# A streaming encoder layer on one NeuronCore: the split weights' homes moved by 16 bytes

## The chip, the cores and the metric

The kernel runs on one core of a Trainium2 chip. The metric is the device time of one execution in microseconds (us). Engines are named as the profile names them: PE (TensorE, matmul), PEld (its weight loads), DVE (VectorE), ACT (ScalarE), POOL (GpSimd), SP (the engine that issues most DMAs). L145 is line 145 of the kernel before.

## The reference, cut to what matters

One layer of a hybrid encoder is computed for 1024 prompt tokens and 64 sample tokens (1088 columns in all) of width 1024, in float32. Each matmul of the reference is dense:

```python
rq, rk, rv, rg, sq, sk, sv, ga, gb = split(rms_norm(x, g_attn) @ w_in)
a = (rms_norm(retention(rq, rk, rv)) * silu(rg)) @ w_ret_out
b = sliding_window_attention(sq, sk, sv) @ w_swa_out
x = x + (sigmoid(ga) * a + sigmoid(gb) * b) @ w_mix_out
x = x + cross_attention(rms_norm(x, g_cross) @ w_cq, mem @ w_mk, mem @ w_mv) @ w_co
x = x + (silu(rms_norm(x, g_ffn) @ w_gate) * (rms_norm(x, g_ffn) @ w_up)) @ w_down
y = rms_norm(x, g_final)
```

Retention keeps a state of 256x256 per head (4 heads) and is worked through in blocks. For the sample tokens the states and key/value caches come in as inputs. The outputs are y, the new states, the last keys and values, and the memory's keys and values.

## The kernel before, in words

**Two parts for each operand.** Float32 operands are split into two parts in the type float32r: `hi`, a rounded copy that ACT writes (L123), and `lo`, the rest, which DVE writes as source minus hi (L124). A product is then three matmuls that add up in PSUM: hi·hi, hi·lo and lo·hi. `mm3` (L147 to L151) does that for one weight block of 128x128 and one stretch of columns.

**Weights.** A weight matrix comes in tiles named `raw` (128 partitions x 1024 numbers, two homes, loaded by SP). The split writes tiles named `wq`, made by `new_op` (L145): 128 partitions x 2 x 512 numbers, the first 512 being hi and the other 512 lo. A pool named "weights" holds the two raw homes and five wq homes in the projection phase and six afterwards. Each 128 columns of a wq tile are the stationary operand of matmuls.

**Strassen.** The large matrices (w_in's parts, w_gate, w_up, w_down) are multiplied by a seven-product scheme. `weight_ops` (L165) forms five of the seven weight sums, with POOL adding and subtracting raw halves in place (L183 to L189), and splits each into a wq tile. `multiply` (L197) is one product: for each of four blocks k of 128 rows it issues six matmuls over 272 columns, two column halves c in two PSUM banks: hi·hi and hi·lo for c = 0, the same for c = 1 (L205, L206 each time), and lo·hi for both (L208). The moving operands are tiles B11, T1 and so on in two rings of eight homes at the right end of SBUF.

**The phases.** `project_phase` multiplies w_in; between its products stands `retention` (L711), head by head, and later `memory_phase` (L485), which computes the memory's keys and values. `mix_phase` does the windowed attention with w_ret_out's products as filler, then w_swa_out and w_mix_out; `cross_phase` and `cross_out_phase` do the cross-attention; `ffn_phase` the gated feed-forward with w_gate, w_up and w_down, and `finish` the last norm.

**Retention's small tiles.** For the sample tokens each head loads kf and qf (128x2x64) and writes sf (64x64). Before, kf shares the home tagged "sf" with the block loop's sf tile, qf has a home tagged "qsm" and the small sf one tagged "sfs" (L777, L790). `bias_table` uses the tag "sf" too.

**The memory phase's small tiles.** Eight pieces of the memory come in through two homes tagged "mraw" (L493); results leave through four homes tagged "mo" (L490).

**What sets the order.** The program is written as a list of steps in Python; the tile framework's scheduler simulates a timeline and orders the instructions of each engine, except where `issue_after` fixes a place. So a tile with another home, or one that shares a home, can change the order. SBUF homes are given out in steps of 32 bytes per partition; in the built program of before, the raw homes start at bytes 8128 and 12224 and the wq homes at 16320, 20416, 24512, 28608, 32704 and (the sixth) 36800. All of these leave the remainder 0 when divided by 64. The ring tiles all leave 32, retention's tiles 0.

Of the kernel before, what the change touches and what calls it, by code (L numbers as in the profile page):

```python
# [11 lines left out]
F32 = mybir.dt.float32  # L12
F32R = mybir.dt.float32r
# [6 lines left out]
P = 128  # L20
# [3 lines left out]
SMP = 64  # L24
# [6 lines left out]
NMEM = 256  # L31
# [78 lines left out]
class Kernel:  # L110
# [31 lines left out]
        return parts  # L142

    def new_op(self):
        return self.wp.tile([P, 2, 512], F32R, tag="wq", bufs=self.wbufs, name="wq")  # L145

    def mm3(self, ps, wh, wl, xh, xl, start, stop):  # L147
        mm = self.nc.tensor.matmul
# [333 lines left out]
    def memory_phase(self, mp):  # L482


        nc, tc, io = self.nc, self.tc, self.io  # L485
        g_mem = self.gains[:, 4, :]
        mr = self.mem.enter_context(tc.tile_pool(name="mr", bufs=1, reuse_waits="tile", side="right"))
        ms = self.ms = [mr.tile([P, 2, NMEM], F32R, name=f"ms{k}") for k in range(KT)]
        macc = mp.tile([P, NMEM], F32, name="macc")
        out = lambda: mp.tile([P, NMEM], F32, tag="mo", bufs=4, name="mo")  # L490
        room = lambda: mp.tile([P, 1024], F32, tag="mw", bufs=3, name="mw")
        for k in range(KT):
            x = mp.tile([P, NMEM], F32, tag="mraw", bufs=2, name="mraw")  # L493
            self.load(x, io["memT"][:, k, :])
            self.gained(ms[k], 0, NMEM, x, g_mem, k)
            if k:
                nc.scalar.activation(x, x, AF.Square)
                nc.vector.tensor_tensor(out=macc, in0=macc, in1=x, op=ALU.add)
            else:
                nc.scalar.activation(macc, x, AF.Square)  # L500
            if k % 2:
                yield
        self.token_rstd(self.mtok, [macc], self.spans(NMEM), D)
        yield
        self.spread(macc, self.mtok)
        for m in range(KT):
            ps = self.dense(self.unit(io["w_mk"][m], KT, room=room), ms, 0, NMEM)
            o = out()
            nc.vector.tensor_tensor(out=o, in0=ps, in1=macc, op=ALU.mult)
            self.store(self.d_mk[m // 2, :, m % 2, :], o)  # L510
            self.store(io["o_mk"][m], o)
            yield
        for h in range(H - 1):
            us = [self.unit(io["w_mv"][h, i], 4, 256, room) for i in range(2)]
            for t in range(2):
                ps = self.dense_psum()
                for k in range(KT):
                    x = ms[k][:, :, t * P:(t + 1) * P]
                    self.mm3(ps[:, :256], x[:, 0], x[:, 1], *us[k // 4][k % 4], k == 0, k == KT - 1)
                o = out()  # L520
                nc.scalar.mul(o, ps[:, :256], self.mtok[:, t:t + 1])
                self.store(self.d_mv[h, :, t, :], o)
                self.store(io["o_mv"][t * P:(t + 1) * P, h * 256:(h + 1) * 256], o)
            yield
# [177 lines left out]
    def retention(self, h):  # L702
        nc, io = self.nc, self.io
        mm = nc.tensor.matmul
        ra = self.ra
# [7 lines left out]
        for b in range(NBLK):  # L713
# [28 lines left out]
            sf = ra.tile([P, BLK + P], F32, tag="sf", bufs=1, name="sf")  # L742
# [31 lines left out]
        self.store(io["o_rsp"][h].rearrange("(t p) e -> p t e", p=P), state)  # L774

        s0, vf = new("state"), new("vf")
        kf, qf = (ra.tile([P, 2, SMP], F32, tag=tag, bufs=1, name=tag) for tag in ("sf", "qsm"))  # L777
        self.load(s0, io["cstate"][h].rearrange("(t p) e -> p t e", p=P))
        vf = vf[:, :, :SMP]
        for j, x in ((1, kf), (2, vf), (0, qf)):  # L780
# [6 lines left out]
        pss = self.bank("psss")  # L787
        for dt in range(2):
            mm(pss[:SMP, 0, :SMP], kf[:, dt, :], qf[:, dt, :], start=dt == 0, stop=dt == 1)
        sf = ra.tile([P, SMP], F32, tag="sfs", bufs=1, name="sfs")  # L790
        nc.vector.scalar_tensor_tensor(sf[:SMP], pss[:SMP, 0, :SMP], self.rtok[:SMP, 8:], dm[:SMP, BLK + P:],
                                       ALU.mult, ALU.mult)
        po = self.bank("pos")
# [903 lines left out]
```

## Time and profile before

| what | before |
|---|---|
| time, median of 3 runs | 2240.6 us (2237.51 to 2248.04) |
| the profiled execution's own time | 2239.58 us |
| its span, first to last instruction | 2237.8 us |
| PE busy | 2171.3 us, 97% |
| PEld busy | 2106.8 us, 94% |
| DVE busy | 1600.4 us, 72% |
| ACT busy | 884.7 us, 40% |
| POOL busy | 690.5 us, 31% |
| mean granted PE clock | 0.986 |

In a row of the groups view, "out<-in" names the tiles by the program's names, "x1832" is the count, and the numbers behind the bar are the group's busy time in us and the mean duration of one in ns. Matmuls are pipelined and their ends are modelled: a matmul row of 289 ns does not mean that the next one starts 289 ns later. The distance from one matmul to the next is read from starts. In a timeline row the first number is the start in us, the second the duration in us. In a row of the windows view stand the stretch, its length, the busy time of each engine with its count, the granted PE clock (PEclk) and the DMA engines' share and rate.

### The profile page before, as it was taken

The page shows a single profiled execution, that of the slowest core. Times are in us where ns is not written, and L with a number is a line of the kernel's source. Part 1 is how long each engine was busy: PE and PEld are TensorE (multiplying, and loading weights), DVE is VectorE, ACT ScalarE, POOL GpSimd, SP SyncE. Part 2 cuts the span into 40 slices and gives each one's busy share as a digit, 9 for nine tenths or more (in the row PEclk, how much of TensorE's full clock was granted, in tenths as well). Part 3 has the DMA queues.
Part 4 walks back from the last instruction along what each step waited for, and adds up shares of the span by engine and source line. Part 5 has one row for each costly group of instructions (what it writes and reads, how often), then busy time and mean ns, then how long its engine had stood idle before and what let it go on. Part 6 is the DMA issues. An engine that isn't in the chain of part 4 may idle for free.

```text
span 2237.8 us, 41757 instructions
## 1 busy us (share of the span) xinstructions
PE 2171.3 (97%) x16434; PEld 2106.8 (94%) x16434; DVE 1600.4 (72%) x2655; ACT 884.7 (40%) x1897; POOL 690.5 (31%) x466
## 2 busy tenths in 40 slices
PE   9999999999999989999999999999999999999996
PEld 9899999999999977779999998999999999999986
DVE  8986878676687668876455555668777777778588
ACT  7333333435444355553133333333222222334243
POOL 1441533342253112220000000014555555434462
PEclk9999999999999999999999999999999999999998
DMA  5433345443445475326443112422332332475233
GB/s 205 156 111 110 117 123 137 133 127 113 167 152 178 151 229 169 114 75 208 130 154 107 55 48 65 134 85 88 122 130 101 102 122 89 142 273 182 84 102 109
DMA packets 182599, 290.86 MB, mean 130 GB/s; under 512 B 40290, under 2 KB 110850, under 8 KB 182402
## 3 DMA queue, kind: packets, MB, share of 16 engines
q1 hardware_dynamic: 177794, 279.26, 39.3%
q10 hardware_dynamic: 4608, 8.91, 1.1%
q8 instruction: 130, 2.13, 0.4%
q14 instruction: 67, 0.55, 0.1%
HBM read 196.95 MB, written 91.16 MB: 129 GB/s over the span
## 4 chain that ended last, share of the span: by engine, by line
PE 75%; DVE 7%; DMA 4%; issue 1%; ACT 1%; POOL 1%; SPq 0%; DVEq 0%; ACTq 0%; POOLq 0%
PE pq L208 14%; PE pq L206 14%; PE pq L205 14%; PE pd L149 7%; PE pd L151 7%; PE pd L150 7%; PE pout L1000 1%; DMA hl<-d_op 1%; PE pp L984 1%; DVE wq L124 1%; PE pss L942 1%; DMA ld<-d_swa 1%; DVE B L124 1%; DMA raw<-w_ret_out 1%; PE pk L699 0%
## 5 line engine op out<-in xcount | busy, mean ns | idle before, releaser
L124 DVE TENSOR_TENSOR wq<-raw,wq 128x512 fp32r<-128x512 f32 (+1 forms) x505 | 450.1, 895 | 124.8 <-ACT wq L123 122.6
L123 ACT CAST wq<-raw 128x512 fp32r<-128x512 f32 (+1 forms) x505 | 307.6, 614 | 569.9 <-PE pq L208 262.7
L205 PE MATMUL pq<-T,wq 128*128 128x272 f32 x1832 | 493.9, 289 | 6.2 <-DVE u L252 3.6
L206 PE MATMUL pq<-T,wq 128*128 128x272 f32 x1832 | 493.9, 289 | 0.0
L206 PE MATMUL pq<-B,wq 128*128 128x272 f32 x1592 | 429.3, 289 | 8.4 <-DVE B L124 8.4
L205 PE MATMUL pq<-B,wq 128*128 128x272 f32 x1592 | 426.7, 288 | 0.0
L208 PE MATMUL pq<-T,wq 128*128 128x272 f32 x1832 | 384.4, 290 | 3.4 <-DVE wq L124 3.4
L183 POOL TENSOR_TENSOR raw<-raw 128x512 f32<-128x512 f32 (+1 forms) x59 | 79.4, 1345 | 894.8 <-DVE rs_r L291 483.8
L205 PEld LDWEIGHTS pq<-T,wq 128*128 128x128 f32 x1832 | 346.7, 189 | 7.1 <-DVE u L252 3.7
L206 PEld LDWEIGHTS pq<-T,wq 128*128 128x128 f32 x1832 | 346.8, 189 | 0.3 <-issue 0.3
L208 PE MATMUL pq<-B,wq 128*128 128x272 f32 x1592 | 334.0, 290 | 0.0
L206 PEld LDWEIGHTS pq<-B,wq 128*128 128x128 f32 x1592 | 300.7, 189 | 10.3 <-DVE B L124 10.0
L205 PEld LDWEIGHTS pq<-B,wq 128*128 128x128 f32 x1592 | 300.1, 189 | 0.7 <-issue 0.4
L208 PEld LDWEIGHTS pq<-T,wq 128*128 128x128 f32 x1832 | 292.0, 191 | 4.6 <-DVE wq L124 3.8
L208 PEld LDWEIGHTS pq<-B,wq 128*128 128x128 f32 x1592 | 253.5, 190 | 0.5 <-issue 0.3
L252 DVE TENSOR_TENSOR u<-pq,u 128x544 f32<-128x544 f32 x177 | 127.5, 720 | 111.7 <-PE pq L208 111.1
L186 POOL TENSOR_TENSOR raw<-raw 128x512 f32<-128x512 f32 (+1 forms) x59 | 85.3, 1446 | 125.2 <-DVE wq L124 122.6
L970 POOL TENSOR_TENSOR t<-t,den 128x768 f32<-128x768 f32 (+2 forms) x34 | 47.8, 1406 | 167.7 <-DVE den L968 49.9
L571 DVE TENSOR_TENSOR stage<-pq,u 128x544 f32<-128x544 f32 x112 | 80.3, 717 | 26.6 <-PE pq L208 25.8
L184 POOL TENSOR_TENSOR raw<-raw 128x512 f32<-128x512 f32 (+1 forms) x59 | 89.2, 1512 | 3.7
L1455 POOL TENSOR_TENSOR y<-u,y 128x544 f32<-128x544 f32 x38 | 62.6, 1658 | 72.4 <-DVE y L1453 54.4
L189 POOL TENSOR_TENSOR raw<-raw 128x512 f32<-128x512 f32 (+1 forms) x59 | 83.2, 1411 | 4.4
(373 smaller groups left out, 4674.2 us busy)
## 6 DMA issues: line engine op xcount, KB each, us to landing
hl<-d_op SPq DMA_DIRECT2D x85, 272.0 KB, 4.4
d_qkv<-stage SPq DMA_DIRECT2D x44, 272.0 KB, 2.3
d_op<-stage SPq DMA_DIRECT2D x44, 272.0 KB, 2.1
d_op<-ht SPq DMA_DIRECT2D x44, 272.0 KB, 3.3
raw<-w_gate SPq DMA_DIRECT2D x22, 512.0 KB, 3.5
raw<-w_up SPq DMA_DIRECT2D x22, 512.0 KB, 3.6
d_gate<-stage ACTq DMA_DIRECT2D x32, 272.0 KB, 2.8
raw<-w_down SPq DMA_DIRECT2D x16, 512.0 KB, 4.4
```

The lines of the kernel that those rows point to most:

```text
L123: self.last_cast = self.nc.scalar.copy(hi, src).ins
L124: return self.nc.vector.tensor_tensor(out=lo, in0=src, in1=hi.bitcast(F32), op=ALU.subtract).ins
L149: mm(ps, wh, xh, start=start, stop=False)
L150: mm(ps, wh, xl, start=False, stop=False)
L151: self.last_mm = mm(ps, wl, xh, start=False, stop=stop).ins
L184: tt(out=a21, in0=a21, in1=a22, op=add)
L186: tt(out=a11, in0=a22, in1=a11, op=sub)
L189: tt(out=a12, in0=a12, in1=a11, op=sub)
L205: mm(ps[:, c, :HC], w[:, 0, ks], x[:, 0, cs], start=start, stop=False)
L206: mm(ps[:, c, :HC], w[:, 0, ks], x[:, 1, cs], start=False, stop=False)
L208: self.last_mm = mm(ps[:, c, :HC], w[:, 1, ks], x[:, 0, c * HC:(c + 1) * HC], start=False, stop=stop).ins
L252: add = lambda out, a, b: nc.vector.tensor_tensor(out=out, in0=a, in1=b, op=ALU.add)
```

## The change

The wq tile grows from 1024 to 1032 numbers per partition (32 bytes more), and the parts start four numbers (16 bytes) into it. In the built program of after, the homes lie at 16320, 20448, 24576, 28704, 32832 and 36960, so hi starts at 16336, 20464 and so on. Divided by 64 these leave 16 or 48, in turn; lo lies 2048 bytes behind hi as before. What lies behind the pool of weights moves by 160 bytes in the projection phase and by 192 afterwards; the rings stay where they are.

To make room, the memory phase's input tiles share the four homes of its output tiles, and retention's kf, qf and small sf become parts of one tile in the home "sf".

```diff
     def new_op(self):
-        return self.wp.tile([P, 2, 512], F32R, tag="wq", bufs=self.wbufs, name="wq")
+        q = self.wp.tile([P, 1032], F32R, tag="wq", bufs=self.wbufs, name="wq")
+        return q[:, 4:4 + 1024].rearrange("p (a b) -> p a b", a=2)
...
         for k in range(KT):
-            x = mp.tile([P, NMEM], F32, tag="mraw", bufs=2, name="mraw")
+            x = mp.tile([P, NMEM], F32, tag="mo", bufs=4, name="mraw")
...
-        kf, qf = (ra.tile([P, 2, SMP], F32, tag=tag, bufs=1, name=tag) for tag in ("sf", "qsm"))
+        small = ra.tile([P, 5, SMP], F32, tag="sf", bufs=1, name="small")
+        kf, qf, sf = small[:, :2], small[:, 2:4], small[:, 4]
...
-        sf = ra.tile([P, SMP], F32, tag="sfs", bufs=1, name="sfs")
```

## The prediction

> **What bounds the kernel now.** I read the page first: busy shares, the slices, the chain, the costliest groups.
>
> ```profile
> PE 2171.3 (97%) x16434; PEld 2106.8 (94%) x16434; DVE 1600.4 (72%) x2655; ACT 884.7 (40%) x1897; POOL 690.5 (31%) x466
> PEclk9999999999999999999999999999999999999998
> PE 75%; DVE 7%; DMA 4%; issue 1%; ACT 1%; POOL 1%; SPq 0%; DVEq 0%; ACTq 0%; POOLq 0%
> PE pq L208 14%; PE pq L206 14%; PE pq L205 14%; PE pd L149 7%; PE pd L151 7%; PE pd L150 7%; PE pout L1000 1%; DMA hl<-d_op 1%; PE pp L984 1%; DVE wq L124 1%; PE pss L942 1%; DMA ld<-d_swa 1%; DVE B L124 1%; DMA raw<-w_ret_out 1%; PE pk L699 0%
> L124 DVE TENSOR_TENSOR wq<-raw,wq 128x512 fp32r<-128x512 f32 (+1 forms) x505 | 450.1, 895 | 124.8 <-ACT wq L123 122.6
> L123 ACT CAST wq<-raw 128x512 fp32r<-128x512 f32 (+1 forms) x505 | 307.6, 614 | 569.9 <-PE pq L208 262.7
> L205 PE MATMUL pq<-T,wq 128*128 128x272 f32 x1832 | 493.9, 289 | 6.2 <-DVE u L252 3.6
> L206 PE MATMUL pq<-B,wq 128*128 128x272 f32 x1592 | 429.3, 289 | 8.4 <-DVE B L124 8.4
> ```
>
> PE is busy for 97% of the span at nearly the full granted clock, and the chain that ended last is three quarters PE, nearly all of it matmuls that take wq as weights. The idle times on PE in the groups are a few us. So neither a transfer nor another engine sets the time: it is the number of matmuls times the distance from one to the next. Since a row's duration is a model, I take that distance from starts: the chain within one stretch of the feed-forward phase, and the windows view for its clock.
>
> ```profile
> 1560.30 0.25 PE pq L208 x2
> 1561.04 0.25 PE pq L208 x2
> 1561.79 0.25 PE pq L208 x2
> ...
> 1578.21 0.25 PE pq L208 x2
> ```
>
> ```profile
> 493.10:494.50 1.40, 1.40 (x14) 1.00 0.04 15
> 691.80:700.10 8.30, 8.30 (x73) 1.00 0.84 250
> 1560.00:1600.00 40.00, 40.00 (x324) 1.00 0.39 130
> ```
>
> Between the first and the last of these 25 rows lie 24 turns of six matmuls: (1578.21 - 1560.30) / 24 = 0.746 us, or 124.4 ns for one matmul of 272 columns. In the third window PE has no idle time and the clock is 1.00. The groups count 1832 + 1592 such matmuls on each of three lines, 10,272 in all; at 124.4 ns these are 1278 us, 57% of the span. By the code another 3,264 take wq as weights through mm3 (w_ret_out, w_swa_out, w_mix_out and w_co 576 each, w_cq 768, w_mk 192). So some 13,500 matmuls read weights from the tiles that move, and **one ns on each is 13.5 us, or 0.6%**. That is the question of this change; all else is small beside it.
>
> **The change part by part.** *Instructions.* No matmul, split or byte of DMA is added or removed: the same 505 casts and 505 subtractions fill wq, over as many numbers, and the same matmuls read it.
>
> *Writing the parts 16 bytes further.* DVE reads raw and hi and writes lo. Does the lie of operands matter to it at all in this trace? Where POOL is still, the same subtraction takes:
>
> ```profile
> L124 DVE TENSOR_TENSOR wq<-raw,wq x16: 682/686/693, 1406.9 to 1496.6; 128x512 fp32r<-128x512 f32 x16
> L124 DVE TENSOR_TENSOR B<-xg,B x12: 712/723/726, 1406.3 to 1498.8; 128x544 fp32r<-128x544 f32 x12
> L123 ACT CAST wq<-raw x16: 610/620/624, 1406.1 to 1493.9; 128x512 fp32r<-128x512 f32 x16
> L123 ACT CAST B<-xg x12: 629/644/652, 1405.6 to 1496.7; 128x544 fp32r<-128x544 f32 x12
> ```
>
> The B tiles lie at remainder 32 of 64 and wq at 0, yet 723 - 686 = 37 ns for 32 more columns (1.2 ns each) is near DVE's whole price per column (686 / 512 = 1.3), and on ACT it is 24 ns (0.8; whole price 1.2). No start of a part lies at 16 in this trace, so the price is bounded by the spreads: 11 ns on DVE and 14 on ACT, up or down, 505 times each: 5.6 and 7.1 us. I take 0. Its cover is that DVE and ACT are busy for 72% and 40% and PE hardly waits for them (the waits below); without that cover it would cost those few us at most. The 895 ns of the page's row is the same work beside POOL, which the shift does not touch.
>
> *Reading the weights 16 bytes further.* Weight loads are PEld's, 94% busy beside PE, so a slower load has little room to hide. In before, weights and moving operand of these matmuls start 32 apart (remainders of 64); after, 16 apart. No row shows 16. The nearest rows compare 32 apart with 0 apart, over 256 columns each, at clock 1.00 by the windows above: the memory phase's products (moving ms in ring-like homes at 32, weights wq at 0) and retention's (qs and ks both at 0).
>
> ```profile
> 691.85 0.28 PE L150 MATMUL pd<-ms,wq 128*128 128x256 f32 x1
> ...
> 700.03 0.28 PE L151 MATMUL pd<-ms,wq 128*128 128x256 f32 x1
> ```
>
> ```profile
> 493.12 0.28 PE L149 MATMUL pss<-qs,ks 128*128 128x256 f32 x1
> ...
> 494.43 0.28 PE L151 MATMUL pss<-qs,ks 128*128 128x256 f32 x1
> ```
>
> The first pair are 70 steps (72 matmuls, the pair being the second and the last): 8.18 us / 70 = 116.9 ns. The second are 11 steps: 1.31 us / 11 = 119.1 ns. So the lie within 64 bytes goes with 2.2 ns a matmul, in a case with the same column count (DMA was busy in the first window and idle in the second, which is the wrong way round to explain it). That is my price for either sign: 13,500 x 2.2 ns = 30 us. Which value to take? The row that is nearest to it is before itself. Its six-matmul turns keep 0.746 us while the weights pass through homes at all distances above 64 bytes from the moving tiles, so bits above 64 do nothing; and 16 lies between 0 and 32 in steps, nearer to neither. I take **0, bounds -30 and +30 us**.
>
> The Trainium skill, SBUF — State Buffer, section Specifications, says that SBUF works in lines of 16 bytes and that crossing into a new one costs. A start moved by one whole line crosses as many lines as before, so by that rule the term is 0; but by it the lies 0 and 32 would cost the same too, and the trace has 119.1 against 116.9 ns, so I keep the bounds.
>
> *The order of instructions.* In the built program only two places are reordered. In head 0 of retention (near 100 to 170 us) PE takes the block's score and output matmuls up to some twenty matmuls later or earlier between the products, with DVE and ACT steps and a w_q load on SP moving along. PE's waits there:
>
> ```profile
> PE pb L823 <- ACT ret_o L819: 4.1, 2, 2.6
> PE pss L149 <- ACT qs L123: 1.2, 1, 1.2
> ```
>
> They may go, or come twice: 5.3 us either way; I take 0, since the steps are moved both forward and back. In the memory phase, ACT, DVE and SP alone are reordered.
>
> *Shared homes.* qf's load now waits, like kf's, for the last reader of the block's sf, and follows kf's on SP's queue.
>
> ```profile
> L117 SPq DMA_DIRECT2D qsm<-d_qkv x4: 360/374/388, 100.4 to 457.8; - x4
> L117 SPq DMA_DIRECT2D sf<-d_qkv x1: 360/360/360, 547.0 to 547.0; - x1
> L789 PE MATMUL psss<-qsm,sf x16: 222/222/270, 211.7 to 563.9; 128*64 128x64 f32 x16
> ```
>
> In head 3 the qf load moves from 457.8 to beside kf's at 547.0, and its first reader starts at about 563.7: some 16 us of slack, and what stands behind it on SP (the store of the state, the next raw loads) is put back by one issue of 0.37 us. Head 0 has more slack, its reader at 211.7. In the memory phase the inputs get four homes in place of two, so their loads can run further ahead; the price is that the first results must find a home free:
>
> ```profile
> L498 DVE TENSOR_TENSOR macc<-macc,mraw x7: 411/419/1082, 619.0 to 664.7; 128x256 f32<-128x256 f32 x7
> ```
>
> The last input is read at 665 us and the first product that writes a result starts after 691 us. Both sharings: 0 us; their worst is one landing late in one place, 3 us.
>
> **The sum.** 2239.58 (the profiled execution; its span is 2237.8, with 1.8 around it, and the runs' median 2240.6 lies 1.0 above) + 0 for writing + 0 for the matmuls + 0 for the order + 0 for the homes: **2240 us**. Its own range, with the order, the homes and the writing: 2230 to 2250.
>
> **The rivals.** *Slower: the weight load pays for a start off 32 bytes.* Place: each of 13,500 loads behind PEld's 94%. For it: every tile of before starts at a multiple of 32, so an unaligned start has never been paid, and the lie of operands does go with 2.2 ns. Against: 0 and 32 apart are both multiples of 32 and say nothing of 16. Price at the row's 2.2 ns: 2240 + 30 = 2270. It decides from 0.8 ns a matmul on (11 us, 0.5%).
>
> *Faster: the shift keeps weight load and moving stream out of each other's way.* For it: if the step from 0 to 32 apart took 2.2 ns off, another lie may take as much off again: 2240 - 30 = 2210. Against: 32 apart may already be the best. The Trainium skill, TensorE: Matmul & The Clock Gate, section Back-to-back issue gap, gives for a lone matmul at full clock its columns over 2.4 plus 2.5 ns: for 272 columns an estimated 115.8 ns, where the trace has 124.4, so by that rule up to 8.6 ns could be there to win; no run here shows how.
>
> *The change does nothing to PE, but the order does.* Then the sum holds with the 5.3 us above: 2234 to 2245, within the forecast.
>
> **How the numbers follow.** The forecast has 0.42, the slower rival 0.31, the faster one 0.27. About 0.5% (11 us) is what a measurement of this kernel can tell from no change. The forecast's own range stays inside 11 us, so the chances are 0.27 faster, 0.42 same, 0.31 slower. For 8 in 10 the range takes in both rivals' prices with a little of their spread: 2208 to 2276.
>
> **What would show it.** In the profile after: the turn of six matmuls in the feed-forward phase, 0.746 us if I am right, 0.76 (six times 2.2 ns more) for the slower rival and 0.733 for the faster; the subtraction of wq beside a still POOL at 686 ns and the cast at 620; retention's matmuls at 119.1 ns (both operands move by 32 there). PE's waits in head 0 within 5 us. I am wrong in kind if the time moves while the turn stays, for then a wait has come that I did not see; or if DVE's subtraction grows to several hundred ns more and PE begins to wait for wq.

## The result, and the profile after

| kernel | median of the runs | ratio to before, 95% interval |
|---|---|---|
| before | 2241.95 us (2237.51 to 2248.04, 10 runs) | |
| after | 2249.35 us (2245.84 to 2255.36, 10 runs) | 1.0031 [1.0021, 1.0041] |

The change makes the kernel slower by 7.4 us, 0.31%. The profiled execution of after took 2255.36 us, the longest of its ten; its span is 2253.5 us and its granted clock 0.986 on the mean, the same as before's. The lines of its page that answer to those of before (from `new_op` on, every line number is one higher):

```profile
PE 2181.9 (97%) x16434; PEld 2118.7 (94%) x16434; DVE 1596.6 (71%) x2655; ACT 885.2 (39%) x1897; POOL 688.8 (31%) x466
PEclk9999999999999989999999999999999999999998
PE 79%; DVE 11%; DMA 4%; issue 2%; ACT 2%; POOL 1%; SPq 0%; DVEq 0%; ACTq 0%; POOLq 0%
L123 ACT CAST wq<-raw 128x512 fp32r<-128x512 f32 (+1 forms) x505 | 307.8, 614 | 579.0 <-PE pq L209 280.6
L124 DVE TENSOR_TENSOR wq<-raw,wq 128x512 fp32r<-128x512 f32 (+1 forms) x505 | 446.9, 889 | 117.7 <-ACT wq L123 115.3
L206 PE MATMUL pq<-T,wq 128*128 128x272 f32 x1832 | 499.3, 291 | 7.0 <-DVE u L253 3.6
L207 PE MATMUL pq<-B,wq 128*128 128x272 f32 x1592 | 432.1, 290 | 6.3 <-DVE B L124 6.3
```

The number of matmuls is the same, and PE is busy for 10.6 us more (2181.9 against 2171.3). DVE and ACT take as long as before. So two thirds of the 15.7 us between the two profiled spans went into PE's busy time. The other 5.1 us are idle time on PE, most of it between 750 and 1010 us, in the windowed attention: 15.8 us idle there where before has 11.2. The kernels w0 and size below, which have the same order of instructions and are as slow by their medians, have 11.8 there, so these waits belong to this execution, 6 us above the median, more than to the change. Of the waits that had been in doubt, those in head 0 of retention are 5.7 us where they were 5.3.

```profile
PE pss L150 <- ACT qs L123: 3.6, 1, 3.6
PE pb L824 <- ACT ret_o L820: 2.1, 2, 1.4
```

The chain, in the stretch of the feed-forward phase that the prediction used, and below it the windows view of the same 40 us (the stretch and its length, then PE, PEld, DVE, ACT and POOL, then the clock and the DMA share and rate):

```profile
1560.40 0.25 PE pq L209 x2
...
1599.52 0.25 PE pq L209 x2
```

The windows view:

```profile
1560.00:1600.00 40.00, 40.00 (x322) 40.00 (x321) 28.41 (x35) 11.88 (x20) 21.87 (x16) 1.00 0.31 98
```

Between the first and the last of 53 rows lie 52 turns of six matmuls: 39.12 / 52 = 0.7523 us, or 125.4 ns for a matmul, where before had 0.746 us and 124.4 ns. PE has no idle time and the clock is 1.00 in both; in 40 us it gets through 322 matmuls where it got through 324. What before did not have is a spread within the stretch:

```profile
1572.45 0.25 PE pq L209 x2
1573.19 0.25 PE pq L209 x2
1573.94 0.25 PE pq L209 x2
1574.69 0.25 PE pq L209 x2
...
1581.46 0.25 PE pq L209 x2
1582.21 0.25 PE pq L209 x2
1582.98 0.25 PE pq L209 x2
1583.74 0.25 PE pq L209 x2
```

Each group of four is one product, that is one weight tile in one home. Three turns of the first take 2.24 us (124.4 ns a matmul), three of the second 2.28 us (126.7 ns). By the addresses in the built program, the first product's weights stand in the home at 20464 and the second's in that at 36976.

Sorted by the home, each distance has its own mean. I took, from the starts of the matmul records, the last twelve steps from one start to the next in each product of 24 matmuls, and wrote beside them how far the moving tile stands behind the weights, modulo 256. All ring tiles are at 224 modulo 256, so the home decides:

| home of hi in after | 16336 | 20464 | 24592 | 28720 | 32848 | 36976 |
|---|---|---|---|---|---|---|
| moving minus weights, modulo 256 | 16 | 240 | 208 | 176 | 144 | 112 |
| mean ns of one matmul | 125.2 | 124.6 | 125.7 | 125.5 | 126.1 | 127.1 |

In before all six homes are 4096 bytes apart, a multiple of 256, so every product has the same 32 and all but a few the same 124.4 to 124.5 ns. In after the homes are 4128 bytes apart, and each has another distance.

This distance is that of the tiles' starts. In one turn the six matmuls begin 0, 2176, 1088, 3264, 0 and 1088 bytes into their block of the moving tile, which is 0, 128, 64, 192, 0 and 64 modulo 256, while the weights they use lie multiples of 512 apart. So the operands themselves have four distances within every turn, and the figures here are means over whole turns: in before, the mean steps at the six places of a turn go from 122.0 to 127.9 ns.

### The profile page after: what moved, and what is told of

Its sections match the earlier page's. It is cut to its first block, busy times and chain, and to the rows that moved or that the text cites. A ratio compares the mean times of both kernels' runs of the same rounds, so it can differ in the third digit from the quotient of the medians.

```text
span 2253.5 us, 41766 instructions
## 1 busy us (share of the span) xinstructions
PE 2181.9 (97%) x16434; PEld 2118.7 (94%) x16434; DVE 1596.6 (71%) x2655; ACT 885.2 (39%) x1897; POOL 688.8 (31%) x466
## 4 chain that ended last, share of the span: by engine, by line
PE 79%; DVE 11%; DMA 4%; issue 2%; ACT 2%; POOL 1%; SPq 0%; DVEq 0%; ACTq 0%; POOLq 0%
PE pq L206 15%; PE pq L209 15%; PE pq L207 15%; PE pd L150 8%; PE pd L151 8%; PE pd L152 8%; DVE wq L124 2%; PE pout L1001 1%; DMA hl<-d_op 1%; PE pp L985 1%; PE pss L943 1%; DMA swin<-d_gate 1%; DVE B L124 1%; DVE T L124 1%; DMA qs<-d_qkv 1%
```

## The experiments

Three theories. **A**: the start of the weights within 64 bytes counts (the prediction's slower rival). **B**: the new order of instructions and the shared homes cost the time. **C**: the distance between weights and moving tile modulo 256 sets the distance from one matmul to the next; the larger tiles, not the 16 bytes, spread the homes over worse distances. "272" below is the mean distance in time over all pairs of matmuls of 272 columns that follow each other in a trace (some 7,600 of the 10,272; gaps left out): 124.60 ns in before, 125.41 in after. Taken over all 10,100 or so pairs without a gap, no kernel's mean differs from the one given by more than 0.15 ns.

### The start within 64 bytes (w0, w16, w32, w48)

Weight tiles of 1040 numbers, so that every home has the same remainder of 64, with the parts at 0, 16, 32 and 48 bytes; the rest as in the change.

```diff
-        q = self.wp.tile([P, 1032], F32R, tag="wq", bufs=self.wbufs, name="wq")
-        return q[:, 4:4 + 1024].rearrange("p (a b) -> p a b", a=2)
+        q = self.wp.tile([P, 1040], F32R, tag="wq", bufs=self.wbufs, name="wq")
+        return q[:, 0:1024].rearrange("p (a b) -> p a b", a=2)
```

(w16 begins at number 4, w32 at 8, w48 at 12.)

> Change's order of instructions and shared homes, but each wq tile 64 bytes larger and its parts at remainder 0 of 64, as before the change. Theory A (the start of the weights against the 64 bytes sets the distance from matmul to matmul): like before, 2242 us, and the turn of six matmuls 0.7467 us. Theory B (the new order and the shared homes cost the 7.4 us, not the shift): 2249 us.

> The same program with every wq part at remainder 16 (the change alternates 16 and 48). Theory A: like the change, 2249 us, each 272-column matmul some 0.8 ns later than before. Theory B: 2249 us as well, whatever the remainder.

> The same program with every wq part at remainder 32, where the moving ring tiles lie too (0 apart). Theory A, form 1 (only a start off 32 bytes is paid): 2242 us. Theory A, form 2 (the distance to the moving operand within 64 bytes is paid, 0 apart being the dearest): retention's 119.1 against 116.9 ns makes 13,500 x 2.2 ns = 30 us, 2272 us. Theory B: 2249 us.

> The same program with every wq part at remainder 48. Theory A, both forms: as w16, 2249 us, within 3 us. Theory B: 2249 us.

| | w0 | w16 | w32 | w48 |
|---|---|---|---|---|
| us | 2249.27 | 2249.86 | 2247.81 | 2248.95 |
| ratio | 1.0033 [1.0022, 1.0044] | 1.0034 [1.0022, 1.0047] | 1.0022 [1.0011, 1.0033] | 1.0036 [1.0024, 1.0047] |
| 272, ns | 125.49 | 125.52 | 125.35 | 125.39 |

w0 has the remainder 0 that before has, and is as slow as the change. The chain of w0 in the feed-forward phase (53 rows, 52 turns of 0.7535 us):

```profile
1560.35 0.26 PE pq L209 x2
...
1599.53 0.24 PE pq L209 x2
```

**A falls.** B stands, since all four have the change's order and homes. These kernels also show more distances (their homes are 4160 apart): at 64 the last twelve matmuls of a product take 123.9 ns, less than before's; at 0, 48, 80, 96, 128, 160 and 192 between 125.4 and 126.0 on the mean. Two of w0's homes have before's distance, 32, and yet a mean of 125.2: of 105 products there whose 24 matmuls follow each other unbroken, 60 stand at 124.4 or 124.5 ns, as in before, and 36 at 126.2 or 126.3, where before has 4 of 325. So where distances are mixed, products at a good one can be slow too; why, no run shows.

### Shared homes without larger tiles (share), larger tiles without the shift (size)

```diff
 share:
-        q = self.wp.tile([P, 1032], F32R, tag="wq", bufs=self.wbufs, name="wq")
-        return q[:, 4:4 + 1024].rearrange("p (a b) -> p a b", a=2)
+        return self.wp.tile([P, 2, 512], F32R, tag="wq", bufs=self.wbufs, name="wq")
 size:
-        return q[:, 4:4 + 1024].rearrange("p (a b) -> p a b", a=2)
+        return q[:, 0:1024].rearrange("p (a b) -> p a b", a=2)
```

> This kernel keeps the shared homes and the moved head-0 retention of the change and takes back its larger weight tiles: the six homes are 4096 bytes apart again and every product has its moving tile 32 bytes behind its weights modulo 256, as in the kernel before. Theory C (the 7.4 us come from the matmuls, whose distance in time hangs on the distance of the two operands' addresses modulo 256): 2241 to 2243 us, same as before, 272-column matmuls at 124.4 to 124.7 ns on the mean. Theory B (the new order of the head-0 retention and the shared homes cost the 7.4 us): 2248 to 2250 us, with the slower matmuls a by-product of it.

> The change with its 32 bytes larger tiles but without the 16 bytes of shift: the weights' parts start their tiles. The homes are 4128 bytes apart, so the distances modulo 256 are spread out (0, 32, 128, 160, 192, 224), as they are in the change (16, 112, 144, 176, 208, 240). Theory C: 2247 to 2251 us, since the spread and not the shift costs the time; mean of the 272-column matmuls 125.2 to 125.6 ns. If the start of the weights off 32 bytes within their 64 were what costs (the prediction's rival): 2240 to 2243 us. Theory B: 2248 to 2250 us.

share took 2240.86 us, ratio 0.9999 [0.999, 1.0008], 272 at 124.59 ns. size took 2251.98 us, 1.0045 [1.0033, 1.0057], 125.53 ns. Both have the change's instructions in the change's order. The chain of share, in 20 us, has 26 turns of 0.7465 us where size, in 40 us, has 52 of 0.7535; share's rows:

```profile
1560.02 0.25 PE pq L209 x2
...
1579.43 0.25 PE pq L209 x2
```

size's rows:

```profile
1560.14 0.25 PE pq L209 x2
...
1599.32 0.26 PE pq L209 x2
```

**B falls**: order and shared homes cost nothing that these runs can tell (the interval is 0.1% to either side). The 32 bytes in the size of the tile are enough for the whole loss, and in size there is no shift at all. The spread does not act through worse distances alone: in size, too, a home has before's 32, and of its 55 unbroken products 15 stand at 126.2 or 126.3 ns.

### All homes moved together (pad224, pad64)

Weight tiles as in share, with unused bytes ahead of everything on the weights' side (56 numbers, or 16).

```diff
+            cp.tile([P, 56], F32, name="pad")
             self.ident = cp.tile([P, P], F32, name="ident")
```

> Weights' tiles as before (4096 bytes apart), shared homes and new order, and 224 bytes of unused room ahead of them: all six homes move together, so that every product has its moving tile 64 bytes behind its weights modulo 256. In an earlier run of mixed distances this one had the shortest matmuls (123.8 ns). Theory C: 0.6 ns less for each of 10,300 272-column matmuls than before, about 2234 to 2238 us. Theory B: 2248 to 2250 us.

> As the kernel with 224 bytes of unused room, but with 64: every product has its moving tile 224 bytes behind its weights modulo 256, a distance at which the change's own spread showed matmuls of about 126 ns. Theory C: 1.2 to 1.6 ns more for each of 10,300 matmuls than before, 2252 to 2258 us. Theory B: 2248 to 2250 us, as all kernels with the shared homes.

pad224 took 2234.13 us, 0.9967 [0.9957, 0.9978], 272 at 123.97 ns: 7.6 us less than before, with nothing but empty room added to share. pad64 took 2250.05 us, 1.0042 [1.003, 1.0054], 126.14 ns: the matmuls as expected, the time 2 us less than expected. The chain of pad224 in 20 us of the feed-forward phase, 26 turns of 0.7435 us:

```profile
1560.28 0.25 PE pq L209 x2
...
1579.61 0.25 PE pq L209 x2
```

The chain of pad64 in the same 20 us, 25 turns of 0.760 us:

```profile
1560.36 0.25 PE pq L209 x2
...
1579.36 0.25 PE pq L209 x2
```

The mean granted clock was 0.989 in pad224's profiled execution and 0.988 in pad64's, so the clock does not make the difference.

### The moving tiles moved instead (rpad224, rpad64, both), and no shared homes (down32)

So far the ring tiles stood still, and the place of the weights alone could have been what counts. A pad of n numbers on the other side of SBUF moves the rings:

```diff
+            ctx.enter_context(tc.tile_pool(name="rpad", bufs=1, reuse_waits="tile", side="right")).tile([P, n], F32, name="rpad")
```

rpad224 has n = 56 and rpad64 n = 16; both has n = 8 and pad224's 56 numbers on the weights' side too. down32 is before with two small constant tiles in one, which moves all weights down by 32 bytes:

```diff
-            self.rtok = cp.tile([P, 9], F32, name="rtok")
+            rm = cp.tile([P, 11], F32, name="rm")
+            self.rtok = rm[:, :9]
             nc.vector.memset(self.rtok, 1.0)
-            self.mtok = cp.tile([P, 2], F32, name="mtok")
+            self.mtok = rm[:, 9:]
```

> Weights' homes where they are in the kernel before (all 192 modulo 256), shared homes and new order; 224 bytes of unused room on the other side of the memory move the moving tiles instead, from 224 to 0 modulo 256, so that they stand 64 bytes behind the weights. If the distance of the two operands decides: as the kernel with 224 bytes ahead of the weights, 2232 to 2236 us, 272-column matmuls at 123.9 to 124.1 ns. If the place of the weights alone decides: as the kernel with the shared homes alone, 2240 to 2243 us, 124.4 to 124.7 ns.

> The same with 64 bytes of unused room: weights' homes where they are in the kernel before, moving tiles at 160 modulo 256, 224 bytes behind the weights. If the distance decides: 2248 to 2254 us, 272-column matmuls at 126.0 to 126.4 ns. If the place of the weights alone decides: 2240 to 2243 us and 124.4 to 124.7 ns.

> 224 bytes ahead of the weights and 32 bytes ahead of the moving tiles: both operands have moved against the kernel before, but their distance is its 32 bytes modulo 256 again. If the distance decides: 2240 to 2243 us and 124.4 to 124.7 ns, though the weights stand where the kernel with 224 bytes ahead of them alone took 2234 us. If the place of the weights alone decides: 2232 to 2236 us and 123.9 to 124.1 ns.

> The kernel before with one edit: two small constant tiles (rtok and mtok) are laid into one, which takes 32 bytes less, so that everything behind them, the weights too, stands 32 bytes lower. No home is shared, no order is written differently, the weights' tiles are as before; the moving tiles stand 64 bytes behind the weights instead of 32. If the distance decides: 2232 to 2236 us, faster than both kernels. If the order of the head-0 retention or the shared homes had a part in the 2234 us of the padded kernel: 2238 to 2243 us.

| | moving minus weights | 272, ns | us | ratio |
|---|---|---|---|---|
| rpad224 | 64 | 123.97 | 2237.6 | 0.9983 [0.9971, 0.9994] |
| rpad64 | 224 | 125.81 | 2250.35 | 1.0043 [1.0027, 1.0059] |
| both | 32 | 124.59 | 2243.35 | 1.0011 [0.9999, 1.0023] |
| down32 | 64 | 123.94 | 2235.95 | 0.9976 [0.9964, 0.9988] |

The chains of the four have 27 rows, 26 turns, in these 20 us. That of rpad224:

```profile
1559.99 0.25 PE pq L209 x2
...
1579.32 0.25 PE pq L209 x2
```

That of rpad64:

```profile
1560.00 0.25 PE pq L209 x2
...
1579.58 0.25 PE pq L209 x2
```

That of both:

```profile
1560.28 0.25 PE pq L209 x2
...
1579.69 0.25 PE pq L209 x2
```

That of down32:

```profile
1560.32 0.25 PE pq L208 x2
...
1579.65 0.25 PE pq L208 x2
```

26 turns take 19.33 us in rpad224 and down32, as in pad224; 19.41 in both, as in before and share. So it is the distance of the two operands, not the place of either: the weights of both stand where pad224's do, and its matmuls are share's. Modulo 512 down32 and pad224 stand at 64 and 320, before and both at 32 and 288, so modulo 256 is enough.

At the distance of 224 the picture is less neat: 26 turns take 19.58 us in rpad64, 0.753 us each, where pad64's turns take 0.760. Sorted by product (the last twelve steps, as above), both kernels show the same two paces: of 327 unbroken products, 92 stand at 125.5 or 125.6 ns and 232 at 126.7 in pad64; 233 and 92 in rpad64. So a distance does not always fix one pace. What chooses between the two is open, and with it the difference between 126.14 and 125.81.

The matmuls came out as expected within 0.2 ns; the times of rpad224 and both lie 1.6 and 0.4 us above what was expected. rpad224's profiled execution had a granted clock of 0.982, below those of the kernels so far; its other eleven runs had 0.984 to 0.989, so that does not explain its median, and what does stays open. down32 shows that the gain needs neither shared homes nor another order by hand.

### The shift by itself (u32, u16, u240, u112)

Open was what the 16 bytes do when all homes keep one distance. Here the homes lie without a gap in one tile, which leaves them 4096 apart with any start:

```diff
-        return self.wp.tile([P, 2, 512], F32R, tag="wq", bufs=self.wbufs, name="wq")
+        self.wi += 1; i = 4 + 1024 * (self.wi % self.wbufs)
+        return self.wbig[:, i:i + 1024].rearrange("p (a b) -> p a b", a=2)
...
             self.wp = ctx.enter_context(self.tc.tile_pool(name="weights", bufs=2, reuse_waits="tile"))
+            self.wi = -1
+            self.wbig = self.wp.tile([P, 1024 * bufs + 8], F32R, tag="wbig", bufs=1, name="wbig")
```

u32 begins at number 0 instead of 4; u240 and u112 have 8 and 40 unused numbers ahead. The homes are handed out by count, so some are written again before their last product and those products take a later operand's weights; the instructions are as many and of the same shapes. There are also more waits. So these four are compared with one another only; they have the same order on every engine.

> Control for the next three, which have the same instructions in the same order and the same tiles: all weights' homes lie in one tile, without a gap, so that the homes are 4096 bytes apart and move together; the weights' parts start at 192 modulo 256 and the moving tiles stand 32 bytes behind them, as in the kernel before. The order of the instructions is another than in the kernel before, so the time itself is open, an estimate 2238 to 2250 us; 272-column matmuls at 124.4 to 124.7 ns by the theory of distances.

> The control with one edit: the parts start 16 bytes further, which is the change's shift without the change's spread of the homes. The moving tiles stand 16 bytes behind the weights everywhere. Theory of distances modulo 256, by the matmuls at this distance in the change's spread (125.2 ns): 0.6 to 0.7 ns more for each of 10,300 matmuls, 6 to 8 us over the control. Theory that a start at 16 of 64 does nothing of its own: 0 to 2 us over the control.

> The shifted kernel with 32 bytes of unused room ahead of the weights: the parts start at 48 of 64, the moving tiles stand 240 bytes behind them. Theory of distances, by the 124.6 ns of this distance in the spread: 0 to 2 us over the control, though the parts start off 32. If a start off 32 bytes costs something by itself: the same as the kernel shifted by 16, 6 to 8 us over the control.

> The shifted kernel with 160 bytes of unused room: the parts start at 48 of 64 again, the moving tiles stand 112 bytes behind them, the distance that was slowest in the spread (126.5 and 127.1 ns). Theory of distances: 1.9 to 2.5 ns more for each of 10,300 matmuls than in the control, 20 to 26 us over it. If a start off 32 bytes is what counts: 6 to 8 us over the control, as the kernel shifted by 16.

| | u32 | u16 | u240 | u112 |
|---|---|---|---|---|
| us | 2401.8 | 2408.45 | 2401.26 | 2410.71 |
| over u32 | | +6.7 | -0.5 | +8.9 |
| 272, ns | 124.71 | 125.18 | 124.55 | 127.03 |
| median product, ns a matmul | 124.4 | 125.2 | 124.4 | 127.8 |

The chain of u32 in 40 us of the feed-forward phase, 53 turns of 0.7468 us:

```profile
1699.95 0.25 PE pq L209 x2
...
1739.53 0.25 PE pq L209 x2
```

That of u16, 53 turns of 0.7511 us:

```profile
1700.01 0.25 PE pq L209 x2
...
1739.82 0.25 PE pq L209 x2
```

That of u112, 51 turns of 0.7667 us:

```profile
1700.02 0.25 PE pq L209 x2
...
1739.12 0.25 PE pq L209 x2
```

The chain of u240 has 53 turns of 0.7466 us:

```profile
1699.93 0.25 PE pq L209 x2
...
1739.50 0.25 PE pq L209 x2
```

The matmuls of u16 and u240 came as expected: the shift of 16 bytes costs 0.7 ns a matmul in the chain where it makes the distance 16, and nothing where 32 more bytes make it 240, though the parts start off 32 both times. The medians go the same way (+6.7 and -0.5 us), but u16's five runs (2401.07 to 2412.18) overlap u32's four (2400.70 to 2406.19), so the time alone would not show it. u112's matmuls are the slowest of all, as expected, but its time rose by 8.9 us, where 20 to 26 had been expected. From u32 to u112 PE's busy time rises by 15.2 us. The line of u32's page:

```profile
PE 2220.6 (93%) x16434; PEld 2150.2 (90%) x16434; DVE 1631.1 (68%) x2655; ACT 888.1 (37%) x1893; POOL 729.7 (30%) x466
```

That of u112's page:

```profile
PE 2235.8 (93%) x16434; PEld 2165.0 (90%) x16434; DVE 1630.9 (68%) x2655; ACT 889.6 (37%) x1893; POOL 709.1 (29%) x466
```

The spans are 2399.8 and 2408.5, so PE's idle time falls from 179.2 to 172.7 us: 6.5 us of the longer matmuls are taken up by waits that were there anyway. The granted clock was 0.961 and 0.966. 2.32 ns for 10,272 matmuls would be 24 us, 9 more than PE's busy time rose by. By the starts, the 9,700th matmul of the program comes at 1490.6 us in u32 and at 1488.5 in u112, the 14,000th at 2058.7 and 2066.8, the last at 2385.1 and 2393.8. So the whole loss arises in one stretch, where the clock is 1.00 and PE hardly waits; ahead of it, where nearly half of these matmuls stand, PE has most of its idle time and the clock goes down to 0.88, and nothing is lost. How much of that is the waits and how much the clock was not settled.

## Why the prediction was right or wrong

**The time and the class.** 2240 us was forecast with a range of 2208 to 2276 and 0.42 for a difference within 0.5%; measured were 2249.35 us and 0.31%. The size was near, but the interval of the ratio leaves 1 out: the kernel did become slower, and the forecast's case, no effect on the matmuls, is not what happened. Ten runs of each tell differences of 0.1%, not only the 0.5% that the prediction took for the least. That the time lies in the range is owed to the bounds of 30 us, four times what the change cost, and says nothing for the sum.

**The step that failed** is the term "0, bounds -30 and +30 us" for reading the weights, and in it the sentence "Its six-matmul turns keep 0.746 us while the weights pass through homes at all distances above 64 bytes from the moving tiles, so bits above 64 do nothing". The homes of before are 4096 apart, the ring tiles 8704, which is 34 times 256, and the two blocks in a ring tile 4352, 17 times 256. Modulo 256 the weights were always 32 bytes ahead: the steady turn showed that the pattern repeats with 256 bytes or a fraction of it, and said nothing of the bits between 64 and 256. The wq homes' start bytes, from which this follows, stand in the section on the kernel.

**The size of that term.** By the records, the 272-column matmul took 0.81 ns more in after: 10,272 x 0.81 = 8.3 us (7.7 over all pairs). The 1,536 of 384 columns went from 173.70 to 175.01 ns (2.0 us), the 768 of 256 columns that read wq from 117.3 to 118.7 (1.0 us), those of 320 stayed. The sum of 11.3 us (10.7) agrees with the 10.6 us of PE's busy time. The part of the 384 columns cannot be laid to the distances: share, with before's distances and before's time, has 175.2 ns there. The medians differ by 7.4 us. Over before, after and the twelve kernels up to down32, a straight line through median against 272 gives 7.9 us for a ns (standard error 0.7, correlation 0.96), below the 10.3 of the count; so part of the slower matmuls is absorbed each time, and where, no run shows.

**The slower rival** ended on the right side with the wrong mechanism. Its place was right (the matmuls, through their weights), its cause, a start off 32 bytes, was not: w0 starts at 0 and is slow, u240 starts at 48 of 64 and is not. Its price row was a true sample read in the wrong unit: the memory phase's products are 32 apart modulo 256 and retention's 0, and 0 is slower than 32 for 272 columns too (125.7 against 124.5 ns, 1.2 where the row had 2.2).

**The faster rival** named a thing that exists, and not in this change: "another lie may take as much off again". The distance of 64 does, with 0.6 ns, about a quarter of the 2.2 that the rival counted on. The estimate of 115.8 ns (from the Trainium skill, TensorE: Matmul & The Clock Gate, section Back-to-back issue gap) was reached at no distance tried; the best is 123.9.

**The rule on lines of 16 bytes** (the Trainium skill, SBUF — State Buffer, section Specifications) made, as the prediction read it, a shift by one whole line free. u16 against u32 is that shift, and it costs 0.7 ns a matmul (turns of 0.7511 and 0.7468 us); the measurement decides. The same page, section Who interferes with whom, gives PE independent read ports for the moving operand and for the weights, and has them interfere with nothing. Here the place of one against the other changes the pace, from 123.9 to 127.8 ns; whether the ports, the memory behind them or something else does it, no run here can tell.

**The terms at nothing.** Writing the parts 16 bytes further costs nothing: in after, beside a still POOL, the subtraction takes 684 ns (686 before) and the cast 620 (620).

```profile
L123 ACT CAST wq<-raw x14: 616/620/623, 1413.8 to 1496.7; 128x512 fp32r<-128x512 f32 x14
L124 DVE TENSOR_TENSOR wq<-raw,wq x14: 683/684/693, 1414.6 to 1497.7; 128x512 fp32r<-128x512 f32 x14
```

Order and shared homes cost nothing that the runs can tell: share. Retention's product, both of whose operands move by the same 160 bytes, keeps its 11 steps in 1.31 us, 119.1 ns, in after's timeline:

```profile
494.11 0.28 PE L150 MATMUL pss<-qs,ks 128*128 128x256 f32 x1
...
495.42 0.28 PE L152 MATMUL pss<-qs,ks 128*128 128x256 f32 x1
```

**The mark to look for** was well chosen: a turn of 0.746 us if the forecast held and 0.76 for the slower rival. 0.7523 lies between the two, because it is a mean over six homes, 0.747 in one product shown above and 0.76 in the other.

## What to carry to other kernels

Where PE runs back to back, work out the address of the weights and of the moving tile from the built program and compare their difference modulo 256; if homes rotate, keep them a multiple of 256 apart, so that all products get the same difference, and then try a few differences by moving everything on one side by 32 bytes at a time: the gain (0.3% here) costs no instruction. The distance that is best here, 64, was found for turns of this form and need not be the best for another. A tile that is made a little larger, or one small constant more ahead of the weights, can change the pace of every matmul behind it, so a difference of some tenths of a per cent between two kernels may be an address and nothing that the edit was about. And a steady row proves that something has no effect only if that something varied: look up the addresses before saying that it did.

## What the runs showed of the hardware that was not expected

- The pace of a matmul of 272 columns with weights loaded for each one goes with the difference of the two tiles' starts modulo 256: 123.9 ns at 64, 124.4 at 32 and 240, 125.2 at 16, 125.4 to 126.4 at most others, up to 127.8 at 112. Where all products have one difference, most have the same pace to 0.1 ns (u16: at least eight in ten at 125.2).
- The difference does not fix the pace everywhere: at 224 products stand at one of two paces, 125.6 or 126.7 ns, in two kernels with all products at that difference, and at 32 a product can stand at 126.3 instead of 124.4, rarely in before (4 of 325), often where homes have mixed differences (36 of 105 in w0).
- The columns matter too: 320 columns took 146.4 to 146.9 ns in every kernel.
- Matmuls of 384 columns can settle at one of two paces with the same addresses: those on w_swa_out took 173.3 to 173.8 ns through nearly all of before and 176.7 in share, while those on w_co took 173.3 or 173.4 in both. If all 1,536 went from one to the other, 3.3 ns each, that would be 5 us, an estimate; it was not looked into.
